# Joining the two expert products for the last 40 of 128 expert blocks in a two-layer trunk kernel

## The chip, the cores and the metric

The kernel runs on one core of a Trainium2 chip. The metric is the device time of one execution in microseconds (us); a lower time is better. Three executions were timed, and one more was run with the hardware profiler. The engines are named as the profile names them: PE is TensorE's matrix product and PEld its weight load, DVE is VectorE, ACT is ScalarE, POOL is GpSimd and SP is SyncE, which issues most transfers (its queue is SPq in the rows). SBUF is the on-chip working memory, PSUM the accumulator memory of PE, and DRAM the chip's main memory.

## What is computed

The reference is a trunk of two layers over 512 latent tokens of width 1024 and 256 context tokens. Each layer has a token mixer and then a PEER feed-forward part: for every token and each of 8 heads it picks the 16 best of 128 x 128 = 16,384 experts by product keys, and adds up those experts, each of which is one column of a table U and one row of a table V. Only that second part is touched here.

```
def one_block(hb):                                  # hb: 128 tokens x 1024
    q = (hb @ wq).reshape(t, 8, 2, 128)
    s = jnp.einsum('thsd,hskd->thsk', q, sub_keys)
    v1, i1 = lax.top_k(s[:, :, 0], 16)
    v2, i2 = lax.top_k(s[:, :, 1], 16)
    cand = v1[..., :, None] + v2[..., None, :]      # 256 per head
    best, pos = lax.top_k(cand, 16)                 # and the expert's number eid = i1 * 128 + i2
    gate = jax.nn.softmax(best, axis=-1)
    act = gelu(jnp.einsum('td,thkd->thk', hb, u_tab[eid]))
    return jnp.einsum('thk,thkd->td', gate * act, v_tab[eid])
```

After it each layer adds the result to its input and normalises (the "residual" below).

## The kernel before

**Two ways for the four token blocks.** Of the four blocks of 128 latent tokens, three are done densely: for every one of the 16,384 experts the kernel computes the activation and multiplies it with a gate that is zero nearly everywhere. The fourth block is done by gathers: POOL issues an indirect transfer of 512 KB (tile `gat`, one row of a table per token) 128 times for U and 128 times for V. After a U gather DVE forms a dot product (`gat<-gat,hb`), after a V gather it adds into `gacc`. In each layer there are 256 such gathers, and the code hands them out a few at a time beside the dense work.

**The dense part has three loops** over 128 expert blocks of 128 experts each.

- `dense_u`: SP loads `du` (512 KB), ACT rounds it to `dh`, POOL (blocks 0 to 47) or DVE (the rest) forms the remainder `dl`, PE does 24 products of 128 x 384, ACT applies Gelu into `da`, and SP writes `da` to `acts` in DRAM (192 KB).
- `gates_all`: for each of 24 groups of 16 tokens DVE makes one-hot tables with four operations on 16-bit tiles (`B`, `A`, and `A2` twice), PE multiplies them (32 products of 128 x 128), and ACT copies the result: the part for expert blocks 0 to 31 into a resident tile `W`, the part for the other 96 blocks into `wst`, which SP writes to `rest` in DRAM (768 KB for a group).
- `dense_v`: SP loads `a` from `acts` (192 KB) and `dv` (512 KB), ACT rounds `dv` to `vh`, DVE forms the remainder `vl`, multiplies `a` with the gates, ACT and DVE split `a` into `gh` and `gl`, and PE does 18 products of 128 x 512 into six PSUM accumulators. For blocks 32 to 127 the gates come back from `rest` in six loads `wk` of 3072 KB. The tiles `vh`, `vl`, `gh`, `gl` lie in a region called `hx`, so the trace prints them as `hx<-dv`, `hx<-dv,hx`, `hx<-a`, `hx<-a,hx`.

**What sets the order.** All instructions of an engine run in the order that the program's scheduler has fixed. The class `Order` marks the dense work as main and the gates and gathers as side, which ties each side step to the main block beside which it stands. The first 61 U blocks stand beside the product-key search (`peer_front`: scores, top-k, selection). After it, each third U block gets one gate group, and each U block one or two gathers; in the V loop two blocks out of three that follow one another get one gather each and the third gets two (tables `GSK`, `GU` and `GV` at lines 57 to 59). When the V loop is over, the layer's residual is made; in the second layer that is the program's end, in the first the next layer follows.

Of the kernel before, what the change touches and what calls it, by code (L numbers as in the profile page):

```python
# [36 lines left out]
ND = 3  # L37
VP = (0,)
GH = 4
# [17 lines left out]
GSK = 3  # L57
GV = (1,1,2)
GU = (1,2,1)
# [7 lines left out]
WR = 32  # L67
WK = 16
# [112 lines left out]
class K:  # L181
# [1440 lines left out]
    def gates_all(self, it, gp, W, rest):  # L1622


        nc = self.nc

        def products(g, B, A):
            st = self.t((128, 128 - WR, 16), "wst", 2)
# [17 lines left out]
        for g in range(ND * 8):  # L1646
# [3 lines left out]
            e = self.t(shape, "A", 1, F16)  # L1650
            nc.vector.tensor_tensor(e, pairs(it[0][:, t]), iota, op=OP.is_equal)
            A = self.t([128, 2] + shape[1:], "A2", 2, F16)
# [8 lines left out]
    def dense_u(self, l, h, area, acts):  # L1661

        nc = self.nc
        T = ND * 128
        for c in range(128):
            raw = self.t((128, 8, 128), "du", DUB, F32, area)
            nc.sync.dma_start(raw, self.io["ut"][l, c])
            hi = self.t((128, 8, 128), "dh", 2, F32R, area)
            lo = self.t((128, 8, 128), "dl", 2, F32R, area)
            nc.scalar.copy(hi, raw)  # L1670
            (nc.gpsimd if c < UN else nc.vector).tensor_sub(lo, raw, hi.bitcast(F32))
            ps = self.p()[:, :T]
            for k in range(8):
                self.mm3(ps, (hi[:, k], lo[:, k]), (h[0][k][:, :T], h[1][k][:, :T]), k == 0, k == 7)
            a = self.t((128, T), "da", 3, F32, area)
            nc.scalar.activation(a, ps, AF.Gelu)
            nc.sync.dma_start(acts[c], a)
            yield

    def dense_v(self, l, acts, acc, W, rest, area, other, made):  # L1680

        nc = self.nc
        T = ND * 128
        cut = Region(self.hx(F32).rearrange("p a b c -> p (a b c)"))
        go = Order(self, VO)
        blocks = {}
        for c in range(128):
            if len(blocks) < (128 - WR) // WK and c == (WK // 2 + len(blocks) * WK if len(blocks) < 2 else
                                                        WR + (len(blocks) - 1) * WK):

                m = len(blocks)
                with go.side():
                    blocks[m] = self.t((128, ND * 8, WK * 16), "wk", 2, F32, area)
                    nc.sync.dma_start(blocks[m], rest[:, :, m * WK * 16:(m + 1) * WK * 16].rearrange("g p x -> p g x"))
            if c == 96:
                made()
            for _ in range(GV[c % len(GV)]):
                with go.side():
                    next(other, None)
            main = go.main()  # L1700
            main.__enter__()
            a = self.t((128, T), "a", AB, F32, area)
            nc.sync.dma_start(a, acts[c])
            raw = self.t((128, 1024), "dv", DV, F32, area)
            nc.sync.dma_start(raw, self.io["v"][l, c * 128:(c + 1) * 128, :])
            vh = cut.t((128, 1024), "vh", VH[0], F32R)
            vl = cut.t((128, 1024), "vl", VH[1], F32R)
            nc.scalar.copy(vh, raw)
            (nc.gpsimd if VP[c % len(VP)] and c < 96 else nc.vector).tensor_sub(vl, raw, vh.bitcast(F32))
            if c < WR:  # L1710
                w = W[:, :, c]
            else:
                m = (c - WR) // WK
                w = blocks[m][:, :, (c - WR) % WK * 16:(c - WR) % WK * 16 + 16]
            a3 = a.rearrange("p (g t) -> p g t", t=16)
            nc.vector.tensor_mul(a3, a3, w)
            gh = cut.t((128, T), "gh", GH, F32R)
            gl = cut.t((128, T), "gl", GH, F32R)
            nc.scalar.copy(gh, a)
            nc.vector.tensor_sub(gl, a, gh.bitcast(F32))  # L1720
            for b in range(ND):
                t = slice(b * 128, (b + 1) * 128)
                for x, y, first, last in ((gh, vh, True, False), (gh, vl, False, False), (gl, vh, False, True)):
                    for q in range(2):
                        nc.tensor.matmul(acc[b][q], x[:, t], y[:, q * 512:(q + 1) * 512],
                                         start=c == 0 and first, stop=c == 127 and last)
            main.__exit__(None, None, None)
# [30 lines left out]
    def run(self):  # L1758
# [5 lines left out]
        for l in range(L):  # L1764
# [86 lines left out]
            acts = [self.d([128, ND * 128], "acts", 128) for _ in range(128)]  # L1851
            ar = self.area("hu", side="right")
            hu = ar.__enter__()
# [8 lines left out]
            dd.enter_context(self.phase("wr"))  # L1862
            W = self.t((128, ND * 8, WR, 16), "W")
            rest = self.d([ND * 8, 128, (128 - WR) * 16], "rest")
            wp = ExitStack()
            wp.enter_context(self.phase("wp"))
            self.iota = self.t((128, 128, 2), "iota", 1, F16)
            self.nc.vector.tensor_copy(self.iota, self.iota1[:, :, None].to_broadcast([128, 128, 2]))
            gs = self.gates_all(it, gp, W, rest)
            more = True  # L1870
            k = 0
            go = Order(self, UO)
            while more:
                with go.main():
                    more = next(gu, self) is not self
                k += 1
                if k % GSK == 0:
                    with go.side():
                        next(gs, None)
                for _ in range(GU[k % len(GU)]):  # L1880
                    with go.side():
                        next(gen, None)
            self.run_all(gs)
            wp.close()
            ar.__exit__(None, None, None)

            def made():

                dd.close()
                if not last:  # L1890
                    at = self.tc.cur_priority
                    self.tc.cur_priority += RP
                    with self.phase("rc", s2=6, s4=3, ld=3):
                        self.residual(c1, c2, self.spilled(accs), l, fm, 5, 1, 1.0, 2)
# [140 lines left out]
```

## Time and profile of the kernel before

| | us |
|---|---|
| median of 3 timed executions | 5893.38 |
| lowest and highest of them | 5886.82, 5901.41 |
| the profiled execution | 5876.15 |
| span of the profiled execution | 5874.4 |
| PE busy in the span | 5024.6 (86%) |
| DVE busy | 4256.7 (72%) |
| ACT busy | 1937.6 (33%) |
| POOL busy | 1779.9 (30%) |
| mean rate of all transfers | 240 GB/s |

The profile is of one execution. Times in the rows below count from the start of its span, so that the first layer's gates begin at 2443.9 and the second layer's at 4873.81. A row of a timeline gives the start, the duration, the engine, the line, the operation, the tiles (out<-in), the shape and the count, and in brackets how long the engine was idle before it and which engine's or transfer's end released it. Nearly all instructions are issued by one helper, so all have its line; they are told apart by their tiles. The granted clock is the share of TensorE's full clock (2.4 GHz) that the chip gave; 0.50 is 1.2 GHz.

### The profile page before, as it was taken

Reading aid. Unit: us, or ns where it says so; the run is one execution under the profiler, and the core shown is the slowest. Engines: PE = TensorE matmul, PEld = TensorE weight load, DVE = VectorE, ACT = ScalarE, POOL = GpSimd, SP = SyncE. Lnnn points to the kernel's source line nnn. Section 1 sums busy time; section 2 is a strip of 40 time slices with the busy share of each in tenths; the row PEclk is TensorE's granted clock in tenths of the full one; section 3 lists DMA queues with packets and bytes.
Section 4 is the critical chain, followed back from the end, with each engine's and each line's share of the span. In section 5 each row is a group of like instructions: output and inputs, shape, how many; then the busy total and the mean of one; then the engine's idle time right before and its main releaser. Section 6 shows DMA issues by size and latency. Waiting matters only on the chain. (4 is left out here: it accounts for less than half of the span.)

```text
span 5874.4 us, 76831 instructions
## 1 busy us (share of the span) xinstructions
PE 5024.6 (86%) x26902; PEld 4221.2 (72%) x26902; DVE 4256.7 (72%) x7999; ACT 1937.6 (33%) x3519; POOL 1779.9 (30%) x1290
## 2 busy tenths in 40 slices
PE   8988878987568687899788979999888989988888
PEld 3787755753457577899666768776777979977766
DVE  4655777877788889588677886467565567877777
ACT  2444421321013323344233353332234323433333
POOL 0000354324553774344333300000003443433332
PEclk9999988998679888999899999999998989999999
DMA  6555499788788774699999954333444348999996
GB/s 215 177 166 182 150 330 324 251 277 317 266 278 295 239 228 159 222 349 340 326 318 347 324 177 141 119 114 115 135 125 137 126 140 284 350 330 323 330 339 241
DMA packets 613557, 1410.11 MB, mean 240 GB/s; under 512 B 97968, under 2 KB 221488, under 8 KB 613168
## 3 DMA queue, kind: packets, MB, share of 16 engines
q1 hardware_dynamic: 465712, 868.26, 43.9%
q0 software_dynamic: 147456, 536.94, 26.8%
q8 instruction: 211, 3.46, 0.2%
q14 instruction: 178, 1.46, 0.1%
HBM read 1244.52 MB, written 160.43 MB: 239 GB/s over the span
## 5 line engine op out<-in xcount | busy, mean ns | idle before, releaser
L146 POOL DMA_INDIRECT gat<-in_u,gidx x512 | 678.5, 1325 | 1089.6 <-DVE gat L146 1012.0
L146 POOL DMA_INDIRECT gat<-in_v,gidx x512 | 644.6, 1259 | 906.3 <-DVE gacc L146 779.0
L146 DVE SCALAR_TENSOR_TENSOR gacc<-gat,gact,gacc 128x1024 f32<-128x1024 f32 x508 | 693.2, 1365 | 101.4 <-DMA gat<-in_v,gidx 97.5
L146 PE MATMUL ps<-hx 128*128 128x512 f32 x3072 | 755.5, 395 | 0.0
L146 DVE SCALAR_TENSOR_TENSOR gat<-gat,hb 128x1024 f32<-128x1024 f32 x512 | 617.3, 1220 | 104.7 <-DMA gat<-in_u,gidx 103.4
L146 PEld LDWEIGHTS ps<-hx 128*128 128x128 f32 x3072 | 590.3, 192 | 126.2
L146 PE MATMUL ps<-hx,dh 128*128 128x384 f32 x2304 | 596.9, 340 | 1.9 <-ACT dh L146 1.9
L146 PE MATMUL pa<-hx 128*128 128x512 f32 x1536 | 418.9, 407 | 167.4 <-ACT hx L146 154.4
L146 PE MATMUL ps<-s,s 128*128 128x128 f32 (+3 forms) x2752 | 418.9, 310 | 161.0 <-issue 85.1
L146 PEld LDWEIGHTS ps<-s,s 128*128 128x128 f32 (+1 forms) x2752 | 374.9, 213 | 231.3 <-issue 124.7
L146 PE MATMUL pa<-hx,dh 128*128 128x384 f32 x1792 | 512.3, 356 | 8.9 <-ACT da L146 7.3
L146 ACT CAST dh<-du 128x1024 fp32r<-128x1024 f32 x256 | 268.6, 1051 | 752.3 <-PE ps L146 403.9
L146 PEld LDWEIGHTS pa<-hx 128*128 128x128 f32 x1536 | 295.2, 195 | 245.4 <-ACT hx L146 161.0
L146 PEld LDWEIGHTS ps<-hx,dh 128*128 128x128 f32 x2304 | 417.2, 189 | 4.1 <-ACT dh L146 4.1
L146 PE MATMUL ps<-hx,dl 128*128 128x384 f32 x1152 | 389.7, 339 | 20.7 <-DVE dl L146 20.7
L146 DVE TENSOR_TENSOR hx<-dv,hx 128x1024 fp32r<-128x1024 f32 x256 | 312.9, 1222 | 124.5 <-ACT hx L146 122.3
L146 PE MATMUL ps<-hx,whi 128*128 128x512 f32 x1152 | 386.4, 404 | 12.1 <-ACT whi L146 12.1
L146 ACT CAST xwhi<-xwraw 128x512 fp32r<-128x512 f32 x352 | 217.8, 620 | 514.2 <-PE pa L146 393.8
L146 PE MATMUL pa<-hx,xwhi 128*128 128x512 f32 x1152 | 377.4, 405 | 4.1 <-ACT hx L146 2.1
L146 ACT CAST hx<-dv 128x1024 fp32r<-128x1024 f32 x256 | 268.4, 1049 | 298.3 <-PE ps L146 177.4
L146 ACT CAST whi<-wraw 128x512 fp32r<-128x512 f32 x320 | 197.7, 621 | 488.8 <-PE ps L146 280.2
L146 PE MATMUL pa<-hx,dl 128*128 128x384 f32 x896 | 321.4, 359 | 43.1 <-POOL dl L146 43.1
(281 smaller groups left out, 10108.8 us busy)
## 6 DMA issues: line engine op xcount, KB each, us to landing
du<-in_ut SPq DMA_DIRECT2D x256, 512.0 KB
dv<-in_v SPq DMA_DIRECT2D x256, 512.0 KB
xwraw<-in_w_in SPq DMA_DIRECT2D x272, 256.0 KB
acts<-da SPq DMA_DIRECT2D x256, 192.0 KB
a<-acts SPq DMA_DIRECT2D x256, 192.0 KB
wraw<-in_w_in SPq DMA_DIRECT2D x176, 256.0 KB
xwraw<-in_w_mod SPq DMA_DIRECT2D x160, 256.0 KB
rest<-wst SPq DMA_DIRECT2D x48, 768.0 KB
```

Of the source, the lines that this page charges most:

```text
L146: r = f(*a, **kw)
```

## The change

The blocks are now split at 88 (`128 - WR`, with `WR` = 40). The gates of the last 40 blocks stay resident, in two tiles of three and two parts of eight blocks each (`WT`, `WK` = 8). For U blocks 0 to 87 nothing changes but the step: one gate group is made beside each U block, with two gathers, until all 24 are made. Blocks 88 to 127 then run through a new loop, `dense_uv`, which does U of the next block and V of the current one in turn, with two or three gathers for a block; their activations are not written to DRAM or read back. `dense_v` follows for blocks 0 to 87, with six gathers for seven blocks; what is left of the gathers is done at the end. The gates of those 88 blocks are written as 11 parts of eight blocks (`rest` has the order part, partition, group, value), and read back in 11 loads of 1.5 MiB into the two gate tiles as these come free. The tiles `vh`, `vl`, `gh`, `gl` move out of `hx`, the U loop's area moves to the left side of SBUF, and `GH` falls from 4 to 3. The context's residual of the first layer is attached to V block 48 of 88, where it was 96 of 128.

```
-GSK = 3
-GV = (1,1,2)
-GU = (1,2,1)
+GV = (1,1,1,0,1,1,1)
+GU = (2,)
+GF = (2,3)
-WR = 32
-WK = 16
+WK = 8
+WT = (3, 2, 3, 2, 3, 2, 1)
+WR = sum(WT[:2]) * WK
+MADE = 48
...
-                for out, part in ((W[:, g], r[:, :WR]), (st, r[:, WR:])):
-                    nc.scalar.activation(out[:, :, 4 * n:4 * n + 4], part, AF.Copy, scale=1 / GATE)
-            nc.sync.dma_start(rest[g], st.rearrange("p i t -> p (i t)"))
+                nc.scalar.activation(st[:, :, 4 * n:4 * n + 4], r[:, :N], AF.Copy, scale=1 / GATE)
+                at = N
+                for w in W:
+                    to = at + w.shape[1] * WK
+                    nc.scalar.activation(w[:, :, g, :, 4 * n:4 * n + 4],
+                                         r[:, at:to].rearrange("p (m i) t -> p m i t", i=WK), AF.Copy, scale=1 / GATE)
+                    at = to
+            nc.sync.dma_start(rest[:, :, g].rearrange("m p x -> p m x"), st.rearrange("p (m i) t -> p m (i t)", i=WK))
...
+    def gate_blocks(self, go, W, rest, area):
...
+        for j, n in enumerate(WT):
+            if j and j + 1 < len(WT):
+                tiles.append(self.gate_tile(j + 1, area))
+            for k in range(n * WK):
+                if j and j + 1 < len(WT) and k % 4 == 0 and k // 4 < WT[j + 1]:
+                    with go.side():
+                        nc.sync.dma_start(tiles[j + 1][:, k // 4].rearrange("p g i t -> p g (i t)"), rest[m])
+                    m += 1
+                yield tiles[j][:, k // WK, :, k % WK]
+
+    def dense_uv(self, l, h, area, acc, go, gates, vv, other):
+
+        at = 128 - WR
+        a = self.u_chunk(l, at, h, area)
+        for c in range(at, 128):
+            w = next(gates)
+            self.beside(go, GF[c % len(GF)], other)
+            with go.main():
+                b = self.u_chunk(l, c + 1, h, area) if c < 127 else None
+                self.v_chunk(l, c, a, w, acc, vv, c == at, False)
+                a = b
...
-                k += 1
-                if k % GSK == 0:
-                    with go.side():
-                        next(gs, None)
-                for _ in range(GU[k % len(GU)]):
-                    with go.side():
-                        next(gen, None)
+                        k += 1
+                        with go.side():
+                            next(gs, None)
+                        self.beside(go, GU[k % len(GU)], gen)
...
+                    self.dense_uv(l, hT, hu, acc, go, gates, vv, gen)
...
+                        self.dense_v(l, acts, acc, go, gates, vv, aa, gen, made)
+                        self.run_all(gen)
```

`u_chunk` and `v_chunk` hold the steps of one block that `dense_u` and `dense_v` held before. Three places of the engines' fixed order show what moves.

**DVE in the second layer, where the gates are made.** `dl` is the remainder of a U block, `gat` the dot product of a gather, `B`, `A` and the operations on `gp` are the four of a gate group. Before:

```order
L146 SCALAR_TENSOR_TENSOR gat_44195,gdot_40526<-gat_44195,hb_39696 128x1024
L146 TENSOR_TENSOR B_44232<-it_7897_36835,iota_40490 128x2048
L146 TENSOR_TENSOR A_44234<-it_7896_36834,iota_40490 128x2048
L146 TENSOR_TENSOR dl_44331<-du_44328,dh_44330 128x1024
L146 TENSOR_TENSOR A_9230_44236<-A_44234,gp_36836 128x2048 x2
L146 SCALAR_TENSOR_TENSOR gat_44285,gdot_40526<-gat_44285,hb_39696 128x1024
L146 TENSOR_TENSOR dl_44368<-du_44365,dh_44367 128x1024
L146 SCALAR_TENSOR_TENSOR gat_44322,gdot_40526<-gat_44322,hb_39696 128x1024
```

After:

```order
L149 TENSOR_TENSOR B_41830<-it_8305_37267,iota_40883 128x2048
L149 TENSOR_TENSOR A_9131_41832<-it_8304_37266,iota_40883 128x2048
L149 TENSOR_TENSOR dl_41991<-du_41988,dh_41990 128x1024
L149 TENSOR_TENSOR A_9131_41832<-A_9131_41832,gp_37268 128x2048
L149 SCALAR_TENSOR_TENSOR gat_41886,gdot_40925<-gat_41886,hb_40089 128x1024
L149 TENSOR_TENSOR A_9131_41832<-A_9131_41832,gp_37268 128x2048
L149 SCALAR_TENSOR_TENSOR gat_41889,gdot_40925<-gat_41889,hb_40089 128x1024
L149 TENSOR_TENSOR B_41926<-it_8305_37267,iota_40883 128x2048
L149 TENSOR_TENSOR A_9145_41928<-it_8304_37266,iota_40883 128x2048
```

Before, a gate's four operations are spread over three U blocks; now one gate, two gathers and about one remainder follow one another in every block.

**SP in the second layer's V loop, around a load of gates.** `a` and `dv` are the two loads of a V block. Before:

```order
L146 DMA a_45304<-acts_36863 128x384
L146 DMA dv_45306<-in_v 128x1024
L146 DMA wk_45269<-rest_40486 128x24x256
L146 DMA a_45337<-acts_36864 128x384
L146 DMA dv_45339<-in_v 128x1024
```

After, at the first such load behind the joined loop:

```order
L149 DMA a_46526<-acts_37276 128x384
L149 DMA dv_46528<-in_v 128x1024
L149 DMA s_10522_49348<-in_ln 128x1024
L149 DMA W_9895_46319<-rest_37358 128x3072
L149 DMA a_46560<-acts_37277 128x384
L149 DMA dv_46562<-in_v 128x1024
```

A load of 24 x 256 values for each partition has become one of 3072 in a row, and there are 11 of them where there were six.

**DVE at the end of the second layer.** `hx` with width 1024 is the remainder of a V block, `hx` with width 512 is the residual. Before:

```order
L146 TENSOR_TENSOR s2_9711_48498<-s2_9711_48498,s4_9706_48486 128x512
L146 TENSOR_TENSOR hx_9278_44518<-dv_9700_48443,hx_9278_44518 128x1024
L146 TENSOR_TENSOR hx_9717_48522<-hx_9717_48522 128x512 x4
L146 SCALAR_TENSOR_TENSOR hx_9717_48522<-hx_9717_48522 128x512
L146 TENSOR_TENSOR hx_9717_48522<-hx_9717_48522 128x512
```

After:

```order
L149 SCALAR_TENSOR_TENSOR gacc_45300<-gat_49320,gact_45297,gacc_45300 128x1024
L149 BN_AGGR hx_49386<-hx_49386 128x2
L149 TENSOR_TENSOR hx_49386<-hx_49386 128x512
L149 SCALAR_TENSOR_TENSOR gacc_45300<-gat_49323,gact_45297,gacc_45300 128x1024
L149 TENSOR_SCALAR hx_49386<-hx_49386 128x1
L149 TENSOR_TENSOR hx_49386<-hx_49386 128x512
L149 SCALAR_TENSOR_TENSOR gacc_45300<-gat_49326,gact_45297,gacc_45300 128x1024
L149 SCALAR_TENSOR_TENSOR hx_49386<-hx_49386 128x1
```

Before, the last gather stands well ahead of the last V block, and the fourth token block's residual (`s2`) is finished ahead of it; now 16 V gathers stand behind the last V block's remainder, in turn with the residual of the dense blocks, and the fourth block's residual comes behind them.

## Rows read from the trace of the kernel before

**Rows 1.** Busy time by stage: window, length, PE, PEld, DVE, ACT, POOL, clock, DMA share, GB/s.

```profile
2786.00:3431.00 645.00, 556.61 (x2409) 451.93 (x2407) 492.13 (x632) 211.98 (x289) 206.17 (x163) 0.93 0.90 321
4874.00:5216.00 342.00, 331.53 (x2351) 327.57 (x2351) 295.48 (x352) 145.91 (x313) 148.65 (x95) 0.99 0.95 334
5216.00:5845.00 629.00, 550.00 (x2398) 449.72 (x2395) 475.34 (x594) 206.51 (x278) 195.62 (x159) 0.93 0.90 318
3431.00:3500.00 69.00, 37.70 (x249) 32.87 (x247) 55.25 (x131) 42.29 (x94) 4.98 (x7) 0.80 0.53 173
```

**Rows 2.** The same in stretches of 20 us inside the second layer's V loop.

```profile
5500.00:5520.00 20.00, 20.00 (x90) 16.54 (x89) 18.61 (x22) 7.74 (x10) 9.35 (x7) 1.00 0.94 326
...
5540.00:5560.00 20.00, 10.06 (x45) 8.00 (x43) 9.85 (x11) 2.08 (x3) 6.71 (x6) 0.86 1.05 384
5560.00:5580.00 20.00, 18.39 (x67) 14.52 (x68) 13.39 (x17) 7.26 (x9) 1.95 (x2) 0.80 0.64 213
```

**Rows 3.** Waits of 5230 to 5845: engine, waited for, us in total, times, longest.

```profile
PE pa L146 <- ACT hx L146: 74.3, 8, 13.5
...
ACT hx L146 <- DMA dv<-in_v: 52.6, 15, 15.2
```

**Rows 4.** Timeline of SP's queue around one load of gates, second layer.

```profile
5340.45 0.43 SPq L146 DMA_DIRECT2D wk<-rest  x1
5342.15 10.91 SPq L146 DMA_DIRECT2D a<-acts  x1
```

**Rows 5.** Timeline of PE behind that load.

```profile
5367.86 1.22 PE L146 MATMUL pa<-hx 128*128 128x512 f32 x2 [10.09 <-ACT hx L146]
```

**Rows 6.** Timeline of DVE where the second layer's gates begin.

```profile
4873.81 1.22 DVE L146 TENSOR_TENSOR B<-it,iota 128x2048 f16<-128x2048 f16 x1
4874.94 1.22 DVE L146 TENSOR_TENSOR A<-it,iota 128x2048 f16<-128x2048 f16 x1
4876.08 1.22 DVE L146 SCALAR_TENSOR_TENSOR gat<-gat,hb 128x1024 f32<-128x1024 f32 x1
...
4879.51 2.36 DVE L146 TENSOR_TENSOR A<-A,gp 128x2048 f16<-128x2048 f16 x2
```

**Rows 7.** Timeline of DVE beside U blocks, ahead of the gates.

```profile
4820.28 1.23 DVE L146 TENSOR_TENSOR dl<-du,dh 128x1024 fp32r<-128x1024 f32 x1 [34.19 <-ACT dh L146]
4824.44 1.23 DVE L146 TENSOR_TENSOR dl<-du,dh 128x1024 fp32r<-128x1024 f32 x1 [2.94 <-ACT dh L146]
```

**Rows 8.** Groups by form, 2470 to 2785: count, busy us, mean ns, idle before.

```profile
L146 PE MATMUL ps<-A,B 128*128 128x128 f16 x672 | 42.3, 219 | 0.0
```

**Rows 9.** Timeline of DVE in the V loop, between two loads of gates.

```profile
5793.27 1.23 DVE L146 TENSOR_TENSOR hx<-dv,hx 128x1024 fp32r<-128x1024 f32 x1 [0.34 <-issue]
...
5794.88 1.28 DVE L146 SCALAR_TENSOR_TENSOR gacc<-gat,gact,gacc 128x1024 f32<-128x1024 f32 x1
5796.08 0.55 DVE L146 TENSOR_TENSOR hx<-a,hx 128x384 fp32r<-128x384 f32 x1
5797.35 1.23 DVE L146 TENSOR_TENSOR hx<-dv,hx 128x1024 fp32r<-128x1024 f32 x1 [0.72 <-ACT hx L146]
```

**Rows 10.** Transfers of 2470 to 2785, U with gates: packets, rate, issues and KB.

```profile
DMA packets 33738, 107.74 MB, mean 342 GB/s; under 512 B 3734, under 2 KB 12014, under 8 KB 33710
...
rest<-wst SPq DMA_DIRECT2D x22, 768.0 KB
```

**Rows 11.** Busy time by stage, columns as in Rows 1, end of the second layer's search.

```profile
4760.00:4780.00 20.00, 14.18 (x69) 13.86 (x69) 18.32 (x23) 4.31 (x6) 6.22 (x4) 0.83 0.32 103
4780.00:4800.00 20.00, 15.71 (x77) 15.71 (x78) 5.32 (x10) 4.31 (x6) 6.40 (x4) 0.83 0.29 94
```

**Rows 12.** Timeline, start of the scores in the second layer.

```profile
4464.72 1.22 PE L146 MATMUL ps<-hx,whi 128*128 128x512 f32 x2 [3.82 <-ACT whi L146]
```

**Rows 13.** Timeline of the program's end.

```profile
5845.18 1.07 ACT L146 COPY hx<-pa 128x512 f32<-128x512 f32 x2 [7.07 <-PE ps L146]
...
5868.28 2.75 DVE L146 TENSOR_TENSOR hx<-hx 128x512 f32<-128x512 f32 x4 [0.28 <-ACT hx L146]
```

More of the change, by code (lines that the diff above doesn't have):

```diff
@@ L38 @@
 VP = (0,)
-GH = 4
+GH = 3
 VH = (2,2)
@@ L1659, in gates_all, with u_chunk @@
         products(*made)
-    def dense_u(self, l, h, area, acts):
+    def u_chunk(self, l, c, h, area):
         nc = self.nc
         T = ND * 128
[L1665 to L1677, printed above, removed]
+        raw = self.t((128, 8, 128), "du", DUB, F32, area)
+        nc.sync.dma_start(raw, self.io["ut"][l, c])
+        hi = self.t((128, 8, 128), "dh", 2, F32R, area)
+        lo = self.t((128, 8, 128), "dl", 2, F32R, area)
+        nc.scalar.copy(hi, raw)
+        (nc.gpsimd if c < UN else nc.vector).tensor_sub(lo, raw, hi.bitcast(F32))
+        ps = self.p()[:, :T]
+        for k in range(8):
+            self.mm3(ps, (hi[:, k], lo[:, k]), (h[0][k][:, :T], h[1][k][:, :T]), k == 0, k == 7)
+        a = self.t((128, T), "da", 3, F32, area)
+        nc.scalar.activation(a, ps, AF.Gelu)
+        return a
@@ L1678, in dense_u, with v_chunk @@
+    def dense_u(self, l, h, area, acts):
+        for c in range(128 - WR):
+            self.nc.sync.dma_start(acts[c], self.u_chunk(l, c, h, area))
             yield
-    def dense_v(self, l, acts, acc, W, rest, area, other, made):
+    def v_chunk(self, l, c, a, w, acc, area, first, last):
         nc = self.nc
[L1683 to L1691, printed above, removed]
-                with go.side():
-                    blocks[m] = self.t((128, ND * 8, WK * 16), "wk", 2, F32, area)
-                    nc.sync.dma_start(blocks[m], rest[:, :, m * WK * 16:(m + 1) * WK * 16].rearrange("g p x -> p g x"))
-            if c == 96:
-                made()
-            for _ in range(GV[c % len(GV)]):
-                with go.side():
[L1699 to L1727, printed above, removed]
@@ new lines, in v_chunk, with beside @@
+        nc.scalar.copy(gh, a)
+        nc.vector.tensor_sub(gl, a, gh.bitcast(F32))
+        for b in range(ND):
+            t = slice(b * 128, (b + 1) * 128)
+            for n, (x, y) in enumerate(((gh, vh), (gh, vl), (gl, vh))):
+                for q in range(2):
+                    nc.tensor.matmul(acc[b][q], x[:, t], y[:, q * 512:(q + 1) * 512],
+                                     start=first and n == 0, stop=last and n == 2)
+    def beside(self, go, n, other):
+        for _ in range(n):
+            with go.side():
+                next(other, None)
@@ new lines, in dense_uv, with dense_v @@
+    def dense_uv(self, l, h, area, acc, go, gates, vv, other):
[8 more added lines that the diff above has]
+                a = b
+    def dense_v(self, l, acts, acc, go, gates, vv, area, other, made):
+        N = 128 - WR
+        for c in range(N):
+            w = next(gates)
+            if c == MADE:
+                made()
+            self.beside(go, GV[c % len(GV)], other)
+            with go.main():
+                a = self.t((128, ND * 128), "a", AB, F32, area)
+                self.nc.sync.dma_start(a, acts[c])
+                self.v_chunk(l, c, a, w, acc, vv, False, c == N - 1)
@@ L1850, in run @@
             accx = self.d([128, 1024], "gacc", 4)
-            acts = [self.d([128, ND * 128], "acts", 128) for _ in range(128)]
-            ar = self.area("hu", side="right")
-            hu = ar.__enter__()
+            acts = [self.d([128, ND * 128], "acts", 128 - WR) for _ in range(128 - WR)]
+            rest = self.d([(128 - WR) // WK, 128, ND * 8, WK * 16], "rest")
+            hu = dd.enter_context(self.area("hu"))
             gu = self.dense_u(l, hT, hu, acts)
@@ L1861, in run @@
             gen = self.gather(l, gx, [accx])
[L1862 to L1875, printed above, removed]
-                k += 1
-                if k % GSK == 0:
-                    with go.side():
-                        next(gs, None)
-                for _ in range(GU[k % len(GU)]):
-                    with go.side():
-                        next(gen, None)
-            self.run_all(gs)
-            wp.close()
```

66 lines of the change are left out of this document (48 added, 18 removed).

## Prediction, before the changed kernel was run

> **What bounds the kernel now.** I read the stages first, as windows that begin and end where a loop of layer 2 or layer 1 does [rows 1]. In U with gates (342 us) PE is busy for 331.5 us at a clock of 0.99: PE bounds it, with the transfers close behind at a DMA share of 0.95. In V (629 us in the second layer, 645 in the first) PE is busy for 550, and part of that at the lower of its two clocks, since the mean is 0.93. The short windows tell where V loses: for most of it PE has no gap (20.00 of 20 us, clock 1.00), but around each load of gates it falls to 10.06 us, the transfers run at 384 GB/s, and the next stretch has a clock of 0.80 [rows 2]. The waits name the same thing: PE waits eight times, 74.3 us in all, for ACT's copies, and ACT for `dv` [rows 3]. In SP's queue the `a` behind a load of gates takes 10.91 us to issue [rows 4], and PE stands still for 10.09 us [rows 5]. A V block without that takes 5797.35 - 5793.27 = 4.08 us [rows 9], so 128 of them 522 us: the six loads of 3 MiB and what follows them cost V 629 - 522 = 107 us, some 18 for each.
>
> **The change, part by part.** All for one layer; the profiled execution is 5876 us, 17 under the median of 5893.
>
> *Before the gates.* From the last selection (beside U block 42, by the order) 19 U blocks stand ahead of the first gate operation before and 15 after. A U block takes 4.16 us there, DVE waiting on PE [rows 7]; that is -17 us. Against it, SP now issues five loads of `du` (512 KB each, the last two behind POOL's remainders) ahead of the first query weights: 2.6 MB at 342 GB/s [rows 10] are 7.7 us, with the waits I take 10, and the scores, which begin with PE already waiting for ACT's `whi` [rows 12], come later by that. Ends: -17, if the five loads cost the scores nothing, and +6, if they cost 23, three times their transfer. Taken: -6, the loads at about their transfer time.
>
> *Gates beside every block.* Two operations of one form follow each other after 1.14 us, and the two on `gp` take 2.28 [rows 6]: a gate is 4.56 us of DVE, two gathers 2.29, and by the order 21 remainders stand among 24 gates, 1.0 a block. That is 7.85 us a block, 188 for 24. PE has 4.16 plus a gate's products, 42.3 us for 21 groups or 2.0 [rows 8]: 6.2 a block. So DVE now bounds this stretch and PE idles about 40 us of it. Before, the same gates stood over 67 U blocks where DVE had room. The 47 U blocks left cost 47 x 4.16 = 195.5, the last gate and the filling of the pipeline 6. U with gates comes to 389.5 where it was 342: **+47.5**. The lower end is +41, without the filling, since nothing in the rows follows faster than 1.14; the upper end is the second rival.
>
> *V.* 40 blocks of it run with U. A pair of blocks there has 8.24 us of PE work, DVE some 6.2 (three operations of 1.14, two of about 0.5, 2.5 gathers of 1.2 [rows 9]), and transfers of 2.36 MB plus a few loads of gates, 300 GB/s: PE bounds it, and the saving and reloading of `a` for these blocks is gone. In the other 88 a block loads 1.17 MB with 0.86 gathers, 286 GB/s, and the eight loads of gates left for them raise the mean to 321, under the 342 that U with gates sustains [rows 10]. Four blocks with one load of 1.5 MiB move 6.25 MB, 18.3 us at that rate against 16.3 of PE: 2 us each, 16 in all. Where the joined loop ends, two loads for the final residual that wait for PE stand in SP's order ahead of the next `dv` and `a`: 8 us; 6 more for the joined loop's start. V comes to 522 + 30 = 552 where it was 629: **-77** (645 becomes 568 in the first layer, whose other 16 us are the context's). Ends: 522, no stall; and 522 + 72, if a half-size load costs half of a `wk`'s 18 us, eight times. I take 30, nearer the rows between two loads, where the transfers keep up at 326 GB/s [rows 2].
>
> *The end.* 16 V gathers now stand behind the last V block's remainder, each 1.20 us [rows 9], 19.2; the fourth block's residual, about ten operations of 0.6, stands behind them, +6. Some 4 us of that run under the last block's products and 3.6 in DVE's idle time before its first residual operation; the rest lengthens the chain from 5845.18 on, where DVE has hardly a gap [rows 13]: **+18** in the second layer. In the first, DVE is busy 55 of the 69 us behind V [rows 1] with what PE waits for next: **+15** of the 19. Ends: 5 and 28.
>
> *Small things.* The resident gates take two copies by ACT instead of one; ACT has 146 of 342 us there [rows 1], and it waits for PE. That `hx` is free in V lets the last residual's loads come early; their wait was under 1 us. `GH` of 3 still leaves three blocks between DVE and PE. All of it: nothing.
>
> *Sum.* Second layer: -6 + 47.5 - 77 + 18 = -17.5. First: -6 + 47.5 - 77 + 15 = -20.5. Together **-38 us**: 5838 for an execution like the profiled one, 5855 against the median.
>
> **The rivals.** (1) *The transfers were the whole of it and V loses nothing more.* If 1.5 MiB loads in long runs (12 KB for a partition in place of 1 KB) no longer stop SP's queue, the 30 us in V go in both layers, and the gathers at the end find DVE's gaps in the first: 60 to 70 us more, 5790, still with the gate stretch at 188. For it: PE is at 20.00 of 20 with 326 GB/s [rows 2], more than the mean forecast here. Against: the loads come two or three in succession, four blocks apart, and for these blocks the bytes ask for 384 GB/s.
>
> (2) *Slower: the small packets of the gates' write.* `rest` is now written as 1408 runs of 512 bytes for a group, one group each block; before, it was runs of 6 KB, one group in three blocks, 768 KB each [rows 10]. A block of this stretch moves 512 + 192 + 704 + 1024 KB, 2.49 MB: 7.3 us at 342 GB/s against DVE's 7.85, so there is next to no room. If such a write costs 1.27 times its bytes, transfers bound the stretch; at twice, the block takes 9.4 us, 24 of them +37, both layers +74: 5929. It decides for "slower" at about 1.8 times. For it: `wk`, read in runs of 1 KB, held SP's queue for 10.91 us [rows 4]. Against: the rate while that load ran was 384 GB/s, no lower than elsewhere [rows 2], so runs of 1 KB cost no rate; 512 bytes are one step from there. The Trainium skill, "DMA: Bandwidth & Descriptors", gives under Specifications 512 B as the least transfer at line rate, and under "Why small descriptors are slow" some three cycles for each packet beside 32-byte beats: an estimate by that is (16 + 3) / 16 = 1.19 times, just under where this rival begins; no row of before shows a load of 512-byte runs to test it.
>
> (3) *The clock.* In the gate stretch PE is busy 6.2 of 7.85 us with a gap in every block. Where PE last had gaps like that, at the end of the search, its clock was 0.83 with 14 to 16 busy us of 20 [rows 11]. At 0.83 it still fits: 6.2 / 0.83 = 7.5. At 0.5 throughout a block takes 12.4, +109 a layer: 6070. Since a slower PE fills its own gaps and [rows 2] shows the clock come back when it does, I give this little. The Trainium skill, "TensorE: Matmul & The Clock Gate", section "HAM oscillation — how this bites in real kernels", says that recurring waits leave a matmul kernel on the throttled clock each time; [rows 11] agree in part, with 0.83, not 0.5.
>
> (4) *No change.* V gains, but DVE's stretch of 188 us comes to 195 (half of its operations follow each other after 1.22 us, their busy time, instead of 1.14), and V stalls for 40 us instead of 30: +14 and +20 over both layers, 5889. It is the forecast with two terms in their upper half.
>
> **How the numbers follow.** A measurement of this kernel can tell about 0.3%, 18 us, from no change. The forecast (5825 to 5880) has 0.42; rival 1 (5780 to 5825) 0.18; rival 4 (5876 to 5911) 0.2; rival 2 (5905 to 5950) 0.15; rival 3, 0.05. Likeliest is the forecast, **5855 us**. The range of 5795 to 5920 leaves out most of rival 1's better half, rival 3 and half of rival 2, about 2 in 10. Faster than 5875.7 are nearly all of the forecast and rival 1: 0.59. Within 0.3%: rival 4 and the edges, 0.22. Slower than 5911: 0.19.
>
> **What would show it.** In the changed trace: 24 gate groups in 185 to 195 us with DVE without gaps and PE's busy time near 6.2 of 7.85 (if DVE waits there and the DMA share is at 1.0, it is rival 2; if PE is full at a low clock, rival 3). No wait of PE over 4 us at a load of gates in V, and SP's next issue quick. 40 joined blocks in about 330 us. The second layer's last V product near 5845 - 20.5 - 35.5 = 5789, and some 47 us from it to the end instead of 29. I am wrong in the mechanism if V keeps stops of 10 us, and wrong in the price of the gate stretch if 24 groups take under 165 or over 205 us.

## The result, and the profile after the change

The changed kernel takes 5832.22 us (median of 4 runs, 5820.75 to 5841.78) against 5893.22 (also 4 runs); the ratio is 0.9895 with a 95% interval of 0.9872 to 0.9918. It is faster by about 61 us by the medians, 48 by the two profiled executions (5826.0 against 5874.4 of span): the one of before lay 17 us under its median, the one of after 4. Timed again with the experiments below, on other chips, the kernel before had medians of 5881.89 to 5887.89, so part of the 61 may be its own spread.

Read off the two timelines, in us (a layer's gates begin with its first `B`):

| | before | after | moved |
|---|---|---|---|
| start to first layer's gates | 2443.9 | 2439.6 | -4.3 |
| first layer, gates to last V product | 987.6 | 942.0 | -45.6 |
| from there to the second layer's gates | 1442.3 | 1463.9 | +21.6 |
| second layer, gates to last V product | 971.3 | 933.0 | -38.3 |
| from there to the end of the span | 29.3 | 47.5 | +18.2 |

Two of these rows give back nearly half of what the other three gain. The windows of the second layer answer [rows 1]: gates with U; the rest of U with the 40 joined blocks; the other 88 V blocks (length, PE, PEld, DVE, ACT, POOL, clock, DMA share, GB/s).

```profile
4846.00:5034.00 188.00, 150.64 (x1289) 142.43 (x1290) 187.45 (x212) 92.04 (x322) 78.59 (x47) 0.96 0.96 304
5034.00:5400.00 366.00, 358.98 (x1845) 329.36 (x1845) 276.51 (x362) 129.89 (x184) 152.42 (x116) 0.99 0.88 308
5400.00:5779.00 379.00, 374.23 (x1651) 307.57 (x1650) 291.15 (x350) 141.86 (x188) 88.56 (x82) 1.00 0.90 319
```

In the first, DVE has no gap (187.45 of 188) and PE idles for 37 us; in the others PE is full but for 12 us. A pair of a U and a V block in the joined loop takes 8.24 us, as forecast, and the 40 joined blocks 327 us. The loads of gates in V, which were the trouble in [rows 2, 4, 5], pass without a mark: in the second layer PE waits 3.04 us where the V loop takes over, and never above 0.5 us behind that. SP's queue at two of them, and PE in windows around them:

```profile
5507.87 0.43 SPq L149 DMA_DIRECT2D W<-rest  x1
5509.45 0.33 SPq L149 DMA_DIRECT2D dv<-in_v  x1
...
5524.85 0.48 SPq L149 DMA_DIRECT2D W<-rest  x1
5527.10 0.33 SPq L149 DMA_DIRECT2D dv<-in_v  x1
```

```profile
5500.00:5520.00 20.00, 20.00 (x90) 16.56 (x89) 16.49 (x20) 6.79 (x10) 4.24 (x5) 1.00 0.95 349
5520.00:5540.00 20.00, 20.00 (x94) 16.67 (x93) 15.66 (x20) 8.21 (x11) 6.06 (x5) 1.00 0.98 358
5540.00:5560.00 20.00, 20.00 (x94) 16.70 (x93) 13.55 (x17) 7.60 (x10) 4.53 (x4) 1.00 0.99 366
...
5580.00:5600.00 20.00, 20.00 (x90) 16.57 (x89) 15.92 (x20) 7.22 (x9) 6.66 (x5) 1.00 0.99 389
```

The issue behind a load takes 0.33 us where it took 10.91, PE is at 20.00, and the transfers carry up to 389 GB/s in these windows. What is given back is the work left to the end. DVE some 20 us before the second layer's end, and the 68 us behind V in the first [answering the last of rows 1, and rows 13]:

```profile
5802.29 1.28 DVE L149 SCALAR_TENSOR_TENSOR gacc<-gat,gact,gacc 128x1024 f32<-128x1024 f32 x1 [1.72 <-DMA gat<-in_v,gidx]
5803.49 0.15 DVE L149 TENSOR_SCALAR hx<-hx 128x1 f32<-128x1 f32 x1
5803.56 0.68 DVE L149 TENSOR_TENSOR hx<-hx 128x512 f32<-128x512 f32 x1
5804.15 1.28 DVE L149 SCALAR_TENSOR_TENSOR gacc<-gat,gact,gacc 128x1024 f32<-128x1024 f32 x1
```

```profile
3382.00:3450.00 68.00, 22.09 (x114) 19.33 (x114) 57.21 (x117) 22.77 (x47) 18.53 (x17) 0.60 0.65 215
```

The last `gacc` runs 25.7 us behind the last V product (5804.15 against 5778.5), between the residual's operations. In the first layer DVE's busy time there hardly changes, but PE's falls from 37.70 to 22.09: what PE waits for comes later.

### The profile page after: what moved, and what is told of

The parts are those of the page before. It is cut to its first block, busy times and chain, and to the rows that moved or that the text cites. A ratio compares the mean times of both kernels' runs of the same rounds, so it can differ in the third digit from the quotient of the medians.

```text
span 5826.0 us, 76885 instructions
## 1 busy us (share of the span) xinstructions
PE 5023.1 (86%) x26902; PEld 4218.3 (72%) x26902; DVE 4273.4 (73%) x7999; ACT 1954.2 (34%) x3711; POOL 1758.1 (30%) x1290
## 5 line engine op out<-in xcount | busy, mean ns | idle before, releaser
L149 POOL DMA_INDIRECT gat<-in_v,gidx x512 | 620.2, 1211 | 1020.9 <-DVE gacc L149 893.6
L149 DVE TENSOR_TENSOR vl<-dv,vh 128x1024 fp32r<-128x1024 f32 x256 | 313.5, 1225 | 203.3 <-ACT vh L149 198.2
L149 PE MATMUL ps<-hx,dl 128*128 128x384 f32 x1152 | 389.9, 338 | 20.7 <-DVE dl L149 20.7
L149 ACT CAST vh<-dv 128x1024 fp32r<-128x1024 f32 x256 | 269.2, 1052 | 341.4 <-PE ps L149 241.4
L149 DVE TENSOR_TENSOR xwlo<-xwraw,xwhi 128x512 fp32r<-128x512 f32 x352 | 242.9, 693 | 159.3 <-ACT xwhi L149 144.9
L149 PEld LDWEIGHTS pa<-hx,dh 128*128 128x128 f32 x1792 | 349.6, 202 | 12.6 <-ACT da L149 10.2
L149 PE MATMUL ps<-vl,gh 128*128 128x512 f32 x1024 | 317.3, 391 | 0.0
L149 PE MATMUL ps<-vh,gh 128*128 128x512 f32 x1024 | 317.0, 392 | 0.0
```

Of the source, the lines that this page charges most:

```text
L149: r = f(*a, **kw)
```

## The experiments

All ratios are to the kernel before, timed beside it, with their 95% intervals; 12 more kernels were timed. The table puts the stages beside each other (us; "gates to V" from a layer's first `B` to its last V product, first and second layer; "between" from the first layer's last V product to the second layer's gates; "end" from the last V product to the end of the span).

| kernel | ratio, interval | gates to V | between | end |
|---|---|---|---|---|
| before | 1 | 987.6, 971.3 | 1442.3 | 29.3 |
| after | 0.9895, 0.9872 to 0.9918 | 942.0, 933.0 | 1463.9 | 47.5 |
| lay_before | 0.9938, 0.9921 to 0.9954 | 970.7, 957.4 | 1442.0 | 29.1 |
| half_old | 0.9915, 0.9888 to 0.9942 | 960.4, 948.9 | 1448.9 | 28.3 |
| lay_half | 0.9772, 0.9751 to 0.9792 | 927.7, 912.9 | 1441.8 | 28.3 |
| lay_quarter | 0.9732, 0.9712 to 0.9752 | 911.7, 884.4 | 1442.7 | 34.3 |
| lay_half40 | 0.9800, 0.9780 to 0.9821 | 928.4, 907.2 | 1441.3 | 28.3 |
| lay_best40 | 0.9806, 0.9785 to 0.9828 | 938.5, 908.7 | 1442.0 | 28.4 |
| dense_gates | 1.0090, 1.0073 to 1.0107 | 1019.7, 1004.2 | 1433.1 | 28.7 |
| join_oldlay | 0.9941, 0.9925 to 0.9958 | 959.7, 942.6 | 1455.5 | 48.6 |
| none_left | 0.9826, 0.9810 to 0.9843 | 947.2, 936.8 | 1434.5 | 24.8 |
| one_half | 0.9786, 0.9763 to 0.9809 | 932.2, 917.9 | 1436.4 | 29.4 |
| pool_dl | 1.0021, 1.0008 to 1.0034 | 1061.8, 1075.4 | 1349.1 | 24.5 |
| half_pool | 1.0000, 0.9985 to 1.0016 | 1052.5, 1063.3 | 1349.1 | 29.4 |

**The layout alone, and the change without it.**

```
lay_before = before with
-    nc.sync.dma_start(rest[g], st.rearrange("p i t -> p (i t)"))
+    nc.sync.dma_start(rest[:, :, g].rearrange("m p x -> p m x"), st.rearrange("p (m i) t -> p m (i t)", i=WK))
-    nc.sync.dma_start(blocks[m], rest[:, :, m * WK * 16:(m + 1) * WK * 16].rearrange("g p x -> p g x"))
+    nc.sync.dma_start(blocks[m], rest[m])
...  (and rest declared in that shape)
join_oldlay = after with these lines the other way round
```

> The kernel before with one part of the change: rest is laid out in six parts, written in runs of 1 KB for a group, and each load of gates reads one run of 24 KB per partition. Nothing else moves. Theory A (V lost time because a load of gates in 3072 short runs stops the queue behind it, and beside that because V asks for more bytes than the transfers carry): a V block still moves 1.40 MB and with the gates 1.55 MB in 4.08 us, 380 GB/s against 342 carried, so V falls from 629 to about 580 us, no stop of SP of 10 us is left, and the total falls by 40 to 90 us, to about 0.988 of before. Rival B (only the bytes count): V keeps 620 or more and the total stays within 15 us. Rival C (only the short runs count): V falls to 535 and the total by 160 to 190.

> The changed kernel with that part undone: rest is written in one run of 5.5 KB per partition and group, and a load of gates reads 3072 runs of 512 bytes (half the bytes of the loads before). All else is as in the changed kernel. Theory A: each of the eight loads in V and the three beside the joined blocks stops SP and PE for 5 to 10 us, so V and the joined blocks take 40 to 80 us more per layer than in the changed kernel, 5910 to 5990 in all, at 1.00 to 1.015 of before. Rival B (bytes only): the same as the changed kernel, 0.9895 of before, within 15 us. The gate stretch of 188 us stays as it is under both, since DVE bounds it; if it falls by over 5 us, the 512-byte writes cost something in the changed kernel.

lay_before gains 0.6%. SP is not stopped any more, yet PE still is: SP at one load, and PE in the windows around it.

```profile
5324.51 0.43 SPq L146 DMA_DIRECT2D wk<-rest  x1
5326.21 0.32 SPq L146 DMA_DIRECT2D a<-acts  x1
```

```profile
5320.00:5340.00 20.00, 18.20 (x81) 14.73 (x79) 14.31 (x23) 6.47 (x9) 5.98 (x6) 1.00 0.99 381
5340.00:5360.00 20.00, 13.79 (x41) 10.46 (x42) 11.92 (x16) 4.95 (x7) 5.33 (x5) 0.74 0.88 327
```

The V loop alone, from its first to its last product, is 596.9 us in the second layer; it was 612.0. Theory A had 580, B 620, C 535: A is nearest, but too hopeful. join_oldlay costs 0.46% against the changed kernel, 10 to 18 us a layer between gates and V, where A expected 40 to 80 and B none: short runs cost something there too, a quarter of what A said. What A had wrong is that a stop of SP is a stop of PE. SP is stopped there behind all 22 loads of gates, for 3.94 to 8.19 us, but behind the start of the second layer's V loop PE waits once for 3.60 us and otherwise at most 1.22. At one of the loads:

```profile
5523.53 0.53 SPq L149 DMA_DIRECT2D W<-rest  x1
5525.11 6.61 SPq L149 DMA_DIRECT2D dv<-in_v  x1
```

`a` and `dv` have three buffers each, which is 12 us of PE's work, so PE can go on while SP stands; that is argued, since no run changed the number of buffers. The gate stretch answers the second rival of the prediction, in its windows for join_oldlay (5.5 KB runs; the changed kernel's is the first row shown above):

```profile
4857.00:5045.00 188.00, 150.50 (x1289) 142.26 (x1290) 187.55 (x212) 92.10 (x322) 78.59 (x47) 0.96 0.90 305
```

Same 188 us, same rate; the DMA share is 0.90 where 512-byte runs have 0.96. The small packets cost the transfers 6 points, and no time that these rows show; DVE bounds the stretch.

**The size of a load.**

```
lay_half = lay_before with            half_old = before with
-WK = 16                              -WK = 16
+WK = 8                               +WK = 8
lay_quarter = lay_half with each load cut in two, the second four blocks later
+    nc.sync.dma_start(blocks[m][:, :ND * 4], rest[m][:, :ND * 4])
+    nc.sync.dma_start(blocks[second[1]][:, ND * 4:], rest[second[1]][:, ND * 4:])
lay_half40 = lay_half with WR = 40
```

> The kernel before with the new layout of rest and with loads of half the size (WK = 8: twelve loads of 1.5 MiB where lay_before had six of 3 MiB; rest written in runs of 512 bytes). No joined blocks, gates as sparse as before. In lay_before no load stopped SP any more, yet V took 597 us and PE still stood for some 10 us at several loads. Theory F (a load of 3 MiB takes all transfers for 8 to 9 us, more than the buffers of a and dv cover; one of 1.5 MiB takes half and is covered): V falls from 597 to 560 to 575 and the total to 0.984 to 0.990 of before, so most of the changed kernel's gain in V needs no joined blocks. Rival B' (V asks for 380 GB/s on the mean, so the bytes bound it whatever the size of a load): V stays at 590 to 600, the total at 0.992 to 0.996, and the joined blocks, which need fewer bytes, are what the rest of the gain comes from.

> The kernel before with loads of half the size alone (WK = 8, twelve loads of 1.5 MiB), in the old layout: each load reads 3072 runs of 512 bytes. Fourth corner beside before (3 MiB, 1 KB runs, V 612 to 627 us), lay_before (3 MiB, long runs, 597 to 611) and lay_half (1.5 MiB, long runs, 557 to 568). Theory F (the size of a load is what the buffers don't cover, the runs add some us each): V 570 to 590 in the second layer, 0.983 to 0.990 of before. Rival J (the short runs undo it: each load stops SP's queue as before, twice as often): V 605 or more, the total within 0.5% of before.

> lay_half with each load cut into two of 0.75 MiB, four blocks apart, runs of 6 KB. Same bytes, same layout. Theory F: what V still loses (557 us against 522 of products) falls again, to 538 to 548, the total to 15 to 35 us less than lay_half, 0.972 to 0.975 of before. Rival K (what is left is the mean rate of V, 380 GB/s, and the passage from U to V): V stays within 6 us of 557 and the total within 8 us of lay_half.

> lay_half with the gates of 40 blocks kept in place instead of 32, so that 11 loads are left of 12 and 1.5 MiB less is written and read per layer. Theory F: 5 us of a load's transfer per layer, V 550 to 555, the total 4 to 14 us less than lay_half. Rival: nothing, within 4 us.

This tells where V's time had gone. The V loop of the second layer by kernel, one window each (before, lay_before, half_old, lay_half, lay_quarter in this order):

```profile
5232.00:5845.00 613.00, 546.38 (x2336) 446.33 (x2336) 467.75 (x582) 201.09 (x260) 190.62 (x154) 0.94 0.90 317
```

```profile
5222.00:5820.00 598.00, 552.81 (x2336) 450.48 (x2336) 468.19 (x582) 200.66 (x262) 186.14 (x154) 0.95 0.89 324
```

```profile
5206.00:5801.00 595.00, 547.30 (x2336) 442.53 (x2336) 466.90 (x583) 199.03 (x259) 200.59 (x154) 0.97 0.94 329
```

```profile
5182.00:5738.00 556.00, 538.93 (x2336) 439.02 (x2335) 467.10 (x583) 198.67 (x259) 204.99 (x154) 0.99 0.94 350
```

```profile
5150.00:5680.00 530.00, 526.97 (x2304) 433.05 (x2305) 459.41 (x570) 193.50 (x256) 204.79 (x153) 1.00 0.96 366
```

With 3 MiB, long runs take V from 612 to 597; with short runs, half the size takes it to 595; both together take it to 557, and a quarter of the size to 530, some 8 us above the 522 of the products. PE's idle time in these windows falls with it, 67, 45, 48, 17 and 3 us; the rest is PE's busy time, 546 in before and 527 in lay_quarter for nearly the same products, at a mean clock of 0.94 in the one and 1.00 in the other. Theory F is right on size with long runs, if too careful (lay_half came to 0.977 where it had 0.984 to 0.990, lay_quarter's V to 530 where it had 538 to 548), and wrong on half_old, where it had 570 to 590 (rival J had 605 or more): short runs still stop SP, 7.33 us for half the bytes in the same 3072 runs,

```profile
5256.31 0.43 SPq L146 DMA_DIRECT2D wk<-rest  x1
5258.00 7.33 SPq L146 DMA_DIRECT2D a<-acts  x1
```

so either cause alone keeps most of the loss. PE's waits are not proportional to the stops: all 12 loads of before stop SP for 9.49 to 11.36 us, and PE waits 8.08 to 11.52 at each of the second layer's six; the 24 of half_old stop it for 3.60 to 10.66, and behind the one shown PE's waits come to 4 us. Rivals B' and K, by which V's bytes bound it, fall: the same bytes moved at 366 GB/s in lay_quarter, and behind its first product no wait of PE in V is above 0.9 us. lay_quarter, which has no joined blocks and the old sparse gates, is 2.7% under before and 1.6% under the changed kernel; under lay_half it is 0.4%, with intervals that just touch. Its end is 6 us longer than lay_half's, since the fourth block's residual now falls behind the last V product. lay_half40 is inconclusive: its stages from gates to V are between 0.7 us longer and 5.7 shorter than lay_half's, its timed ratio is larger, and the intervals overlap.

**The dense gates alone.**

```
dense_gates = before with
-GSK = 3
-GU = (1,2,1)
+GSK = 1
+GU = (2,) * 25 + (1,) * 60
```

> The kernel before with only the gates made denser: one gate group and two gathers beside each U block until the 24 are made, then one gather a block. Theory A (DVE bounds that stretch and PE's idle time there is not given back): 24 groups take 186 to 190 us, PE is busy for about 148 of them, U with gates takes 386 instead of 342, both layers +80 to +95 us, 1.014 of before. Rival D (U blocks behind the gates find transfers and DVE free, and V gets a head start, so the idle time is made up): within 20 us of before.

```profile
4906.00:5093.00 187.00, 152.45 (x1285) 143.47 (x1286) 186.24 (x210) 84.45 (x228) 82.19 (x46) 0.95 0.90 310
5093.00:5293.00 200.00, 199.65 (x1165) 199.17 (x1163) 113.81 (x147) 69.19 (x102) 49.43 (x50) 1.00 0.88 299
```

The stretch is 187 us with DVE full (186.24), as theory A had it, and U with gates 386.5. But the layer loses 33 us, not 44: the passage from the last Gelu to the first V product is 8.7 us (5301.4 - 5292.7) where it was 17.2 in before (5233.1 - 5215.9), since the last gates are no longer made there, and V takes 4 us less. In all 0.9%, between the two theories.

**The end, and DVE's stretch.** (`UN` is the U block from which on DVE and not POOL forms the remainder, 48 elsewhere.)

```
none_left = after with GF = (2,3,3), GV = (1,)
one_half = none_left with GU = (1,2), GF = (3,)
pool_dl = none_left with UN = 82 (POOL makes dl up to block 81)
half_pool = one_half with UN = 82
lay_best40 = lay_half40 with
-                if k % GSK == 0:
+                if k * 24 // 64 > (k - 1) * 24 // 64:
```

> The changed kernel with no gathers left to the end: eight gathers for three joined blocks instead of 7.5, and one for each V block instead of six for seven. Theory A: the end of the second layer falls from 47.5 us to about 30 and the stretch between the first layer's last V product and the second layer's gates by some 12 to 18, while V's transfers rise from 317 to 335 GB/s and cost 0 to 8 us a layer: 20 to 35 us less than the changed kernel, 5797 to 5812. Rival E (V and the joined blocks have no room for these transfers, so the gathers cost there what they save at the end): within 10 us of the changed kernel, V 15 us longer.

none_left gains 0.7% over the changed kernel, some 40 us: the end falls from 47.5 to 24.8, "between" from 1463.9 to 1434.5, and V gives back only 4 to 5 us a layer. The 16 gathers left to the end had cost 23 us in the second layer and 29 in the first, more than the 19.2 of their own operations. Rival E falls.

> none_left with 1.5 gathers beside a gate instead of two, and three beside each joined block instead of 2.67. Theory A: DVE needs 4.56 + 1.71 + 1.0 = 7.3 us a block, 24 of them 174 us, 14 less per layer; the joined blocks move 340 GB/s instead of 320 and lose 0 to 6 us a layer: 15 to 28 us less than none_left, about 0.979 of before. Rival H (the joined blocks have no room for it): what the gate stretch gains the joined blocks lose, within 8 us of none_left.

Theory A: 0.9786 where some 0.979 was expected; the gate stretch is 178.4 us (174 had been worked out), a layer 15 to 19 shorter from gates to V, and the joined blocks lose nothing; the end is 4.6 longer.

> none_left with one limit moved: POOL instead of DVE forms the remainder of U blocks up to 81 (UN = 82 for 48), so that DVE has only the gates and two gathers beside a block: 6.85 us where it had 7.85. Theory A (DVE bounds the gate stretch, the transfers at 342 GB/s are next at 7.3 us, PE at 6.2): the stretch falls from 188.5 to 172 to 178 us, both layers 20 to 30 us less than none_left, about 0.978 of before. Rival G (the transfers bound it already, their share is 0.96, or POOL's 2.4 us for a remainder holds up its gathers): the stretch stays within 4 us of 188 and the total within 8 us of none_left.

> Both edits at once: 1.5 gathers beside a gate, and POOL forms the remainders up to block 81. DVE needs 6.3 us a block, PE 6.2, the transfers 2.23 MB or 6.5 us at 342 GB/s. Theory A: the gate stretch falls to 155 to 162 us, 27 to 33 less per layer, and the total to 45 to 62 us less than none_left, about 0.974 of before, a version that beats both kernels. Rivals G and H: no less than the better of the two single edits.

Both failed, and neither theory had it so. The order moved too: the first gates come 64 to 87 us earlier, and "gates to V" is 115 to 145 us longer, 49 to 58 a layer net. In pool_dl DVE makes four operations of the gates and then stands, since POOL, which runs in its own order, issues the first U gather only behind its subtractions:

```profile
4880.46 1.23 DVE L149 SCALAR_TENSOR_TENSOR gat<-gat,hb 128x1024 f32<-128x1024 f32 x1 [90.04 <-DMA gat<-in_u,gidx]
```

From there to the last gate are 225 us where none_left takes 189 for all of it. Groups by form of pool_dl, and below them of none_left, 2470 to 2630 (count, busy us, mean ns, idle before):

```profile
L149 DVE TENSOR_TENSOR A<-A,gp 128x2048 f16<-128x2048 f16 x32 | 51.4, 1607 | 1.1
...
L149 DVE SCALAR_TENSOR_TENSOR gat<-gat,hb 128x1024 f32<-128x1024 f32 x33 | 48.3, 1486 | 12.9 <-DMA gat<-in_u,gidx 12.9
L149 POOL TENSOR_TENSOR dl<-du,dh 128x1024 fp32r<-128x1024 f32 x16 | 45.2, 2824 | 56.2 <-ACT dh L149 56.2
```

```profile
L149 DVE TENSOR_TENSOR A<-A,gp 128x2048 f16<-128x2048 f16 x41 | 50.0, 1219 | 0.0
L149 DVE SCALAR_TENSOR_TENSOR gat<-gat,hb 128x1024 f32<-128x1024 f32 x41 | 49.9, 1218 | 0.0
```

The means, 1607 and 1486 ns instead of 1219 and 1218, mix two kinds. An operation that no subtraction of POOL overlaps still takes 1.21 to 1.30 us, beside a gather's issue too; one that runs beside a subtraction can take up to 3.42:

```profile
4920.56 3.08 POOL L149 TENSOR_TENSOR dl<-du,dh 128x1024 fp32r<-128x1024 f32 x1 [10.24 <-ACT dh L149]
4921.31 3.42 DVE L149 TENSOR_TENSOR B<-it,iota 128x2048 f16<-128x2048 f16 x1
```

How much of the loss is this and how much the moved order wasn't told apart.

> lay_half40 with the gates spread so that the last is made beside U block 125 instead of behind the U loop (three gates for eight blocks instead of one for three). In lay_half 15 to 18 us lie between the last Gelu and the first V product, in dense_gates, where the gates were done early, 8 to 9. Theory: that passage falls to 9 us and the total by 10 to 20 us against lay_half40, about 0.972 of before, the best version so far. Rival: the gates made earlier hold up U as much (DVE), within 5 us.

The passage from U to V fell to 9.8 us as expected, from 20.7 in lay_half40, but U with gates grew from 341.9 to 354.3: the rival.

## Why the prediction came out right, step by step

The sign and the range held (5832 in 5795 to 5920); the size was 38 forecast against 48 between the profiled executions and 61 between the medians. The main mechanism held: DVE bounds the gates, and V loses its stops. The total is nearer than its terms, since V came out 25 us better over both layers than forecast and the first layer's end 14 worse, and two of the terms below are right only in their sums.

- *Before the gates*, -6 forecast: -4.3. Eight kernels with the old front reach the first layer's gates at 2441.4 to 2455.8, mean 2448.4, and four with the new at 2439.6 to 2445.2, mean 2441.8: -6.6. The sum is right, and the spread shows that a single pair could not have told it; but the parts are right only in part. The scores start 12 us later with the new front (mean 1967.8 against 1956.0 in the first layer), where 10 were forecast for the five loads. The stretch from the last selection to the gates, though, which was to lose four U blocks or 17 us, is only 4 to 6 us shorter (74.8 and 90.0 before, 70.4 and 84.3 after), and 58 U blocks are finished when the gates begin in both kernels. The rest came from the search itself, 12 to 16 us shorter from scores to last selection, which I had not forecast and no run explains. That the parts add up to -6 is luck.
- *Gates beside every block*, 188 us bound by DVE: 188.4 and 188.6. Right, with PE busy for 151 us of it (148 forecast). A small slip beside it: the 107 us that I charged to six loads held the 17 us of the passage from U to V; the loads were nearer 90.
- *V and the joined blocks.* From the last gate operation to the last V product 753.5 us were forecast for the second layer and 16 more for the first; 744.4 and 753.6 came. The mechanism holds (no stop at a load), but I gave each load 2 us from a cap of 342 GB/s. That cap was the rate of a stretch that PE bounded; with long runs the same core moved 349 to 389 over 20 us. The whole term was 9 us too large in the second layer and 16 in the first.
- *The end*, +18: +18.2, but by two errors that cancel. Without the 16 gathers (none_left) the end is 24.8 us, 4.5 under before, so the gathers cost 22.7. The 4.5 go with a term that I had put at nothing, the last residual's loads that come early: I had read DVE's own wait for them (0.77 us), while the chain that ends last in before runs through one of them, between the last V product and the residual:

```profile
5846.03 5.54 DMA hx<-x
```

In none_left that chain goes from V straight into DVE's residual. The early loads were not tried alone. *The first layer's end*, +15: about 29 by none_left. I counted the gathers' time on DVE less its idle time there; but they stand in turn with the residual, so each lengthens the chain that PE waits for. The term was half of what it should have been. What the gathers cost beyond their own 19.2 us, and why 29 in the first layer and 23 in the second, was not tested; in the second, the chain that ends last holds two waits for a gather to land, of 6.62 and 7.36 us.
- The rivals: the second (small packets) is answered by join_oldlay, where the stretch keeps its 188 us. An estimate of the price of the 512-byte runs from these rows: the transfers' share rises from 0.90 to 0.96 at the same rate, and 704 of a block's 2432 KB are such runs, so they take some 1.2 times as long, coarsely, since the shares have two digits. My estimate from the Trainium skill, "DMA: Bandwidth & Descriptors", "Why small descriptors are slow", was 1.19 times for the write itself; the trace agrees, and no time hung on it. The third (the clock): 0.96 in the stretch, not 0.83 or 0.5; it falls. The first had V's direction: of its 30 us a layer in V, 9 came in the second layer and 16 in the first, and the total stayed above its 5790, since the gathers at the end kept their price. The fourth did not come.
- What the prediction did not ask: whether the joined blocks are needed. lay_half has the loads' size and layout and nothing else, and is 1.2% under the changed kernel, of which the gathers at the end explain 0.7. The denser gates, which joining needs since all must be done by block 88, cost 32 to 33 us a layer from gates to V (dense_gates, with the old loads). none_left is still 19 and 30 us longer there than lay_half40, which has the same 40 resident blocks, the loads' size and layout, and no joined loop; so the joined loop gives back only some 3 to 13 us of that. That is worked out across kernels, since no run has the joined loop without dense gates. The best joined kernel, one_half, can't be told from lay_half (the intervals overlap).

## What to carry to other kernels

A bulk load that shares a queue with a steady stream should be laid out in long runs and cut until the stream's reader no longer waits at a piece; either alone kept most of the loss here, both took V from 612 to 557 us at half the size and to 530 at a quarter. That the piece must fit under what the stream's buffers cover is how I read it; no run changed the buffers. Before a loop is rebuilt to move fewer bytes, try that first: the mean rate of a stretch that an engine bounds is no limit of the transfers. And work that is spread beside a loop must be counted to its last piece, since 16 pieces left over, 19.2 us of DVE's time, cost 23 and 29 us on the chain behind it. And a stage that comes out as forecast may hide two errors: take the terms apart in a run of their own.

## What had not been expected of the hardware

- A load in many short runs stops SP's queue. 3072 runs held the next issue for 10.91 us with 3 MiB [rows 4], 9.49 to 11.36 at the 12 loads of before, and for 7.33 with 1.5 MiB, 3.60 to 10.66 at the 24 of half_old; 3 MiB in 128 long runs for 0.32 or 0.33 at all 12 of lay_before. So bytes alone don't stop it; with the short runs, both count.
- Such a stop need not reach PE: in join_oldlay SP stands for 3.94 to 8.19 us behind each of 11 loads in a layer, and the layer loses 10 to 18 us in all.
- An operation of DVE beside POOL's subtraction takes up to 3.42 us where it takes 1.22 alone, and the subtraction 2824 ns on the mean where it takes 2.39 us beside an idle DVE; a gather that POOL issues does not lengthen it (at most 1.30). The Trainium skill, "SBUF — State Buffer", section "Who interferes with whom", says that a DVE instruction with two SBUF inputs contends with a GpSimd instruction that reads SBUF; these rows agree with it.
